# Features made one group ahead, a last step without modulation work, and another chain for the norm's scale, in a two-layer decoder trunk

## The chip, the cores and the metric

The kernel runs on one core of a Trainium2 chip. The metric is the device time of one execution, in microseconds. The engines are TensorE (PE in the rows; PEld is its weight load), VectorE (DVE), ScalarE (ACT), GpSimd (POOL) and SyncE (SP), which here issues the transfers.

## What is computed

A decoder trunk of two layers for 256 tokens of 2048 features, in fp32. Each layer has two halves, a mixer (attention) and a squared-ReLU MLP with hidden size 8192. Both halves begin with an RMSNorm whose output is scaled and shifted by a vector that depends on the condition `c`, and end in a residual add with a gate that depends on `c` as well. Cut to this, the reference is:

```python
cond = jax.nn.silu(c)
for i in range(DEPTH):
    mod = cond @ ada_w[i] + ada_b[i]          # ada_w[i] is 2048 x 12288
    sh1, sc1, g1, sh2, sc2, g2 = [m[:, None, :] for m in jnp.split(mod, 6, axis=-1)]
    h = rms_norm(x, norm_mix_g[i]) * (1.0 + sc1) + sh1
    ...
    x = x + g1 * y                            # y: even_mixer or odd_mixer of h
    h = rms_norm(x, norm_mlp_g[i]) * (1.0 + sc2) + sh2
    x = x + g2 * (jnp.square(jax.nn.relu(h @ mlp_up[i])) @ mlp_down[i])
return rms_norm(x, final_norm_g)
```

## The kernel before

`xT` keeps the residual with features on partitions: 16 slices of 128 features by 256 tokens. Every product with a weight matrix is made of three fp32r matmuls. A weight block (`load`, 128 x 1024 elements, 512 KB) is split on the core into a high part `wh` (ACT, L319) and a low part `wl` (DVE, L321); activations are kept as a high and a low part as well (`xs` for a normed input, `hs` for others). Eight buffers hold blocks on their way in, four each hold `wh` and `wl`.

`make_h` (L459) makes the normed features of some slices, three instructions a slice: a product `t` of `xT`, the modulated norm weight and the norm's scale `R` on DVE (L463), its shifted high part on ACT (L464), the low part on DVE (L465).

The modulation vectors come from `ada_w`, a matrix as large as the MLP's. `queue` lines up its column sections in `fill`; `ada` is a generator that does one step for each `pump`: it loads one 512 KB block and accumulates it into a row, on DVE (L242, L245) or, for a few sections, on TensorE (L238). After a section's last step its row is put into `late`, one entry for each 512 columns: four TensorE transposes (L263), a DVE reduction (L265) and small DVE instructions (L272, L275) that write `mod`. `tick`, called with nearly every weight load, first does one entry of `late`, then adds `2 * rate[0]` to a credit and pumps once for each whole unit. `need(left, keys)` pumps until at most `left` sections of the keys are queued, and empties `late`.

The even mixer's input projection (`even`, L615) can't wait for the whole modulation. It runs in five feature groups (`K1_GROUPS`, L39) of 2, 2, 4, 4 and 4 slices. For a group it calls `need`, then `make_h`, and then nine projections with `kproj` (L374): one of keys and values held in two `bank` tiles of PSUM, then pairs for `qb`, `qa`, `ka`, `va`. Partial sums of a group are copied out by ACT (L402) and copied back into PSUM for the next one (L383). The rates of the groups stand in `R_K1` (L41). `up_streamed` (L671) does the same for the first half of the up projection of layer 0: four groups of 4 slices, eight projections each.

`down` (L499) makes output projections in four blocks of 512 features and four steps of 512 rows. With `residual` (L477) it adds into `xT` and, for the next norm, squares each slice on ACT (L147) and adds it on DVE into `sacc` (L151); the last square is kept apart. `sumsq` (L440) sums over features by TensorE, `rstd` (L433) takes the power -0.5 on POOL (L437), and `norm_scale` (L448) spreads the result over all partitions: DVE scales an identity matrix by it (L453), TensorE multiplies by ones (L454) into `R` in PSUM, and ACT copies it to `Rs` in SBUF if `keep` (L456). `Rs` is the same tile as `sacc`.

In layer 1 the features of a norm are made lazily: `lazy_h` (L470) puts four calls of `make_h` into `hgen`, and the first `proj` (L348) after it takes one for each step of 512 rows.

The framework works out waits between engines from the tiles that instructions touch and sets each engine's order of instructions by its own estimates; `tc.issue_after(i)` puts what a block issues behind instruction `i` on its engine.

Of the kernel before, what the change touches and what calls it, by code (L numbers as in the profile page):

```python
# [15 lines left out]
ALU = mybir.AluOpType  # L16
# [24 lines left out]
R_K1 = (0.6, 0.75, 0.9, 0.9, 1.6)  # L41
# [41 lines left out]
def build(tc, consts, x, c, norm_mix_g, norm_mlp_g, ada_w, ada_b, mlp_up, mlp_down, even_w_in, even_sinks,  # L83
# [5 lines left out]
    with ctx:  # L89
# [258 lines left out]
        def proj(W, c0, outs):  # L348
            Ps = []
            off = 0  # L350
            for kind, n, ev in outs:
                Ps.append((off, [mm_tile() for _ in range(n // 128 if kind == "T" else 2)]))
                off += n
            for g in range(4):
# [5 lines left out]
                tick()  # L360
                for (kind, n, ev), (o, P) in zip(outs, Ps):
# [78 lines left out]
        def sumsq():  # L440
            ps = aux()
            sq = last.pop()
            for j in range(2):
                T.matmul(ps[:, j:j + 1], sacc[:, 128 * j:128 * j + 128], ones[:, 0:1], start=True, stop=False)
                T.matmul(ps[:, j:j + 1], sq[:, 128 * j:128 * j + 128], ones[:, 0:1], start=False, stop=True)
            return ps[:, 0:2]

        def norm_scale(ss, keep=True):  # L448
            r = rstd(ss)
            R = aux()  # L450
            dg = t256()
            for j in range(2):
                V.tensor_scalar(dg[:, 128 * j:128 * j + 128], ident, r[:, j:j + 1], None, op0=ALU.mult)  # L453
            T.matmul(R[:, 0:S], ones, dg, start=True, stop=True)  # L454
            if keep:
                A.activation(Rs, R[:, 0:S], AF.Copy)  # L456
            return R[:, 0:S]

        def make_h(l, sh, sc, R, ks=range(KT)):  # L459
            for k in ks:  # L460
                t = t256()
                b = mod[:, 6 * l + sh, k:k + 1]
                V.scalar_tensor_tensor(t, xT[:, k, :], mod[:, 6 * l + sc, k:k + 1], R, op0=ALU.mult, op1=ALU.mult)  # L463
                ia = A.activation(xs[:, k, 0:S], t, AF.Identity, bias=b)  # L464
                iv = V.scalar_tensor_tensor(xs[:, k, S:2 * S], t, b, xs[:, k, 0:S].bitcast(F32), op0=ALU.add, op1=ALU.subtract)  # L465
            return ia, iv
# [3 lines left out]
        def lazy_h(l, sh, sc, R):  # L470
            for g in range(4):
                hgen.append(lambda g=g: make_h(l, sh, sc, R, range(4 * g, 4 * g + 4)))
# [26 lines left out]
        def down(W, row0, tiles, order, ev, lazy=None):  # L499
            for blk in range(4):  # L500
                P = [mm_tile() for _ in range(4)]
                for n, g in enumerate(order):
                    ws = load(W, row0 + 512 * g, 4, 512 * blk, 512)
                    tick()
# [27 lines left out]
        def mlp(l, first=0, us=None):  # L532
            ys = []
            for ch in range(first, 4):
# [24 lines left out]
                down(mlp_down[l], 2048 * ch, tiles, range(4), residual(l, 5, True, l == 1) if ch == 3 else partial(l, ys, ch))  # L559
# [55 lines left out]
        def even():  # L615
# [24 lines left out]
            held = [bank() for _ in range(2)]  # L640
            for g, (k0, kn) in enumerate(K1_GROUPS):
                end = len(K1_GROUPS) - 1
                need(end - g, (0, 1))
                ia, iv = make_h(0, 0, 1, Rs, range(k0, k0 + kn))
# [303 lines left out]
```

## Time and profile before

| what | value |
| --- | --- |
| median of 3 runs | 2288.84 us (2287.96 to 2292.45) |
| the profiled execution | 2290.15 us |
| its span, first to last instruction | 2288.4 us |
| PE busy | 2216.7 us, 97% |
| DVE busy | 1662.1 us, 73% |
| ACT busy | 1180.4 us, 52% |
| moved by DMA | 600.06 MB, mean 262 GB/s |

The windows below give, for a stretch, the busy time of each engine and in brackets its number of instructions, the clock that was granted to TensorE as a share of 2.4 GHz, the busy share of the DMA engines and what they moved. Matmuls are pipelined and their ends are modelled, so their count in a stretch says more than their busy time.

### The profile page before, as it was taken

To read this page: it belongs to the slowest core of one execution; us is meant where nothing else is said; L and a number is where in the kernel's file an instruction comes from. 1 tells how busy PE (TensorE), PEld (TensorE's weight loads), DVE (VectorE), ACT (ScalarE), POOL (GpSimd) and SP (SyncE) were. 2 spreads that over 40 slices of the span, in tenths; PEclk is the share of its full clock that TensorE was granted. 3 is DMA by queue.
4 is the path that set the end of the run, shared out by engine and by line. 5 is a ranking of instruction groups with operands and counts; after the bars stand their busy time and mean duration, and the time that the engine had idled before them with its cause. 6 is when DMAs were issued, how large, how long until landed. Compare 5 with 4: busy or idle time off the path is not lost.

```text
span 2288.4 us, 45838 instructions
## 1 busy us (share of the span) xinstructions
PE 2216.7 (97%) x18602; PEld 2147.1 (94%) x18602; DVE 1662.1 (73%) x2341; ACT 1180.4 (52%) x1873; POOL 5.6 (0%) x25
## 2 busy tenths in 40 slices
PE   8899999899999999999999999999999999999998
PEld 4799889899999999999999989899999999999997
DVE  3887899988877788887777977887545555555555
ACT  3766974578844354354454555444444444443543
POOL 0000000000000000000000000000000000000000
PEclk9999999999999999999999999999999999999999
DMA  9999679999998988988858876985555656555652
GB/s 320 312 333 322 242 258 364 326 355 364 328 317 276 319 290 300 312 306 295 262 184 296 313 253 222 325 313 159 193 198 190 199 190 201 188 198 189 199 185 93
DMA packets 296246, 600.06 MB, mean 262 GB/s; under 512 B 24706, under 2 KB 41954, under 8 KB 296034
## 3 DMA queue, kind: packets, MB, share of 16 engines
q1 hardware_dynamic: 295488, 596.38, 76.5%
q8 instruction: 146, 2.39, 0.4%
q10 hardware_dynamic: 546, 0.75, 0.1%
q14 instruction: 66, 0.54, 0.1%
HBM read 594.95 MB, written 2.10 MB: 261 GB/s over the span
## 4 chain that ended last, share of the span: by engine, by line
PE 47%; issue 33%; DVE 8%; DMA 7%; ACT 4%; SPq 0%; DVEq 0%; POOLq 0%; POOL 0%; ACTq 0%
PE mm L333 30%; PE mm L399 12%; DMA wa<-in_ada_w_dram 5%; DVE wl L321 3%; DVE acc L245 2%; PE bank L399 1%; ACT wh L319 1%; DMA w<-in_odd_w_in_dram 1%; PE row L238 1%; DMA w<-in_even_w_in_dram 1%; PE cps L263 1%; ACT u L402 1%; ACT mm L383 0%; PE bank L605 0%; ACT hs L417 0%
## 5 line engine op out<-in xcount | busy, mean ns | idle before, releaser
L321 DVE TENSOR_TENSOR wl<-w,wh 128x1024 fp32r<-128x1024 f32 x736 | 881.6, 1221 | 421.3 <-ACT wh L319 417.2
L319 ACT ACTIVATE wh<-w 128x1024 fp32r<-128x1024 f32 x736 | 754.1, 1055 | 771.4 <-PE mm L333 666.6
L333 PE MATMUL mm<-hs,wh 128*128 128x256 f32 x5120 | 881.3, 277 | 0.4 <-DVE xT L481 0.4
L333 PEld LDWEIGHTS mm<-hs,wh 128*128 128x128 f32 x5120 | 772.6, 188 | 1.6 <-DVE xT L481 1.0
L333 PE MATMUL mm<-xs,wh 128*128 128x256 f32 (+1 forms) x4128 | 717.8, 279 | 3.1 <-ACT xs L464 3.0
L333 PE MATMUL mm<-hs,wl 128*128 128x256 f32 x2560 | 708.3, 277 | 4.1 <-DVE wl L321 4.1
L333 PEld LDWEIGHTS mm<-xs,wh 128*128 128x128 f32 (+1 forms) x4128 | 626.3, 188 | 6.4 <-ACT xs L464 4.5
L333 PE MATMUL mm<-xs,wl 128*128 128x256 f32 x2064 | 571.7, 278 | 0.4 <-DVE wl L321 0.3
L245 DVE SCALAR_TENSOR_TENSOR acc<-wa,cond,acc 128x1024 f32<-128x1024 f32 x330 | 423.1, 1282 | 98.1 <-DMA wa<-in_ada_w_dram 96.3
L333 PEld LDWEIGHTS mm<-hs,wl 128*128 128x128 f32 x2560 | 481.0, 188 | 5.1 <-DVE wl L321 4.9
L333 PEld LDWEIGHTS mm<-xs,wl 128*128 128x128 f32 x2064 | 387.6, 188 | 1.5 <-DVE wl L321 1.0
L399 PE MATMUL mm<-xs,wh 128*128 128x256 f32 x1792 | 315.2, 280 | 6.0 <-ACT wh L319 4.2
L399 PEld LDWEIGHTS mm<-xs,wh 128*128 128x128 f32 x1792 | 273.2, 190 | 16.4 <-ACT wh L319 5.4
L399 PE MATMUL mm<-xs,wl 128*128 128x256 f32 x896 | 249.1, 279 | 1.5 <-DVE wl L321 1.5
L399 PEld LDWEIGHTS mm<-xs,wl 128*128 128x128 f32 x896 | 169.2, 190 | 2.2 <-DVE wl L321 2.1
L402 ACT ACTIVATE u<-mm 128x512 f32<-128x512 f32 x144 | 84.1, 592 | 73.9 <-PE mm L399 73.0
L383 ACT ACTIVATE mm<-u 128x512 f32<-128x512 f32 x112 | 65.5, 597 | 1.2
L548 ACT ACTIVATE t<-mm 128x256 f32<-128x256 f32 x96 | 36.5, 380 | 31.5 <-PE mm L333 26.2
L147 ACT ACTIVATE t<-xT 128x256 f32<-128x256 f32 x60 | 24.6, 415 | 51.3 <-DVE xT L481 51.3
L577 ACT ACTIVATE p<-p,st 128x128 f32<-128x128 f32 (+1 forms) x96 | 40.1, 420 | 19.7 <-DVE st L591 10.0
L399 PE MATMUL mm<-wh,xs 128*128 128x256 f32 x256 | 49.4, 286 | 0.1
L343 PE MATMUL mm<-wh,xs 128*128 128x256 f32 (+1 forms) x128 | 43.7, 342 | 0.0
(213 smaller groups left out, 1408.4 us busy)
## 6 DMA issues: line engine op xcount, KB each, us to landing
wa<-in_ada_w_dram SPq DMA_DIRECT2D x256, 512.0 KB, 5.2
w<-in_mlp_up_dram SPq DMA_DIRECT2D x256, 512.0 KB, 4.4
w<-in_mlp_down_dram SPq DMA_DIRECT2D x256, 512.0 KB, 4.9
wa<-in_ada_w_dram SPq DMA_DIRECT2D x256, 256.0 KB, 5.1
w<-in_odd_w_in_dram SPq DMA_DIRECT2D x88, 512.0 KB, 4.7
w<-in_even_w_in_dram SPq DMA_DIRECT2D x72, 512.0 KB, 5.4
w<-in_even_w_out_dram SPq DMA_DIRECT2D x32, 512.0 KB, 5.7
w<-in_odd_w_out_dram SPq DMA_DIRECT2D x32, 512.0 KB, 5.5
```

Of the source, the lines that this page charges most:

```text
L147: A.activation(s, xT[:, kt, :], AF.Square)
L238: T.matmul(row[q:q + 32, :], cond[:, k:k + 1].to_broadcast([128, 32]), w[:, i, :], start=k < 4, stop=k >= KT - 4, tile_position=(0, q))
L245: V.scalar_tensor_tensor(acc, w[:, i, :], cond[:, k:k + 1], acc, op0=ALU.mult, op1=ALU.add)
L319: A.activation(wh, w, AF.Copy)
L321: V.tensor_tensor(wl, w, wh.bitcast(F32), op=ALU.subtract)
L333: T.matmul(P[0:m, 0:S], st[:, c0:c0 + m], mv, start=f and i == 0, stop=e and i == 2)
L343: T.matmul(Ps[j][:, 0:n], lo, wh[:, c0:c0 + n], start=False, stop=e)
L383: A.activation(P, flat[i], AF.Copy)
L399: T.matmul(Ps[i][:, 256 * h:256 * h + 256], st, mv, start=first and e == 0, stop=last and e == 2, skip_group_check=True)
L402: A.activation(flat[i], P, AF.Copy)
L548: A.activation(r, P[:, 0:S], AF.Relu)
L577: A.activation(p[:, o:o + n], p[:, o:o + n], AF.Exp, bias=m[:, i:i + 1], accum_out=den[:, i:i + 1])
```

## The change

- `even` and `up_streamed` get a function `features(g)` with the `need` and the `make_h` of a group. Group 0's is called first. Group g+1's is called inside group g: in `even` before the last two projections (`ka`, `va` of b = 1) of a 2-slice group, before the last (`va`) of a 4-slice group; in `up_streamed` before the eighth.
- The first two rates of `R_K1` become 0.65 and 0.9.
- `down` takes `sums`; where a sum of squares follows, the last step of the last block calls no `tick`.
- `sumsq` multiplies both halves of `sacc` first, then both halves of the last square, as one accumulation.
- `norm_scale` no longer scales an identity on DVE: TensorE takes the broadcast result of POOL as the stationary operand, against the identity. The copy to `Rs` is always made, and layer 1's groups after the first read `Rs`.
- `make_h` puts each product from the third on behind the low part two slices before it.
- In the first `proj` after `lazy_h`, the first step goes slice by slice through its four output tiles, and no longer tile by tile through its four slices.

```diff
-R_K1 = (0.6, 0.75, 0.9, 0.9, 1.6)
+R_K1 = (0.65, 0.9, 0.9, 0.9, 1.6)
...
+            fresh = len(hgen) == 4
             for g in range(4):
...
                 tick()
+                if fresh and g == 0:
+                    for k in range(4):
+                        for mt in range(4):
+                            mm_T(Ps[0][1][mt], ws[k:k + 1], 128 * mt, 128, xs_rhs(k, 1), k == 0, False)
+                    continue
...
         def sumsq():
             ps = aux()
             sq = last.pop()
-            for j in range(2):
-                T.matmul(ps[:, j:j + 1], sacc[:, 128 * j:128 * j + 128], ones[:, 0:1], start=True, stop=False)
-                T.matmul(ps[:, j:j + 1], sq[:, 128 * j:128 * j + 128], ones[:, 0:1], start=False, stop=True)
+            for t in (sacc, sq):
+                for j in range(2):
+                    T.matmul(ps[:, j:j + 1], t[:, 128 * j:128 * j + 128], ones[:, 0:1], start=t is sacc and j == 0, stop=t is sq and j == 1,
+                             skip_group_check=True)
...
-        def norm_scale(ss, keep=True):
+        def norm_scale(ss):
             r = rstd(ss)
             R = aux()
-            dg = t256()
             for j in range(2):
-                V.tensor_scalar(dg[:, 128 * j:128 * j + 128], ident, r[:, j:j + 1], None, op0=ALU.mult)
-            T.matmul(R[:, 0:S], ones, dg, start=True, stop=True)
-            if keep:
-                A.activation(Rs, R[:, 0:S], AF.Copy)
+                T.matmul(R[:, 128 * j:128 * j + 128], r[:, j:j + 1].to_broadcast([128, 128]), ident, start=True, stop=True)
+            A.activation(Rs, R[:, 0:S], AF.Copy)
...
         def make_h(l, sh, sc, R, ks=range(KT)):
+            done = []
             for k in ks:
                 t = t256()
                 b = mod[:, 6 * l + sh, k:k + 1]
-                V.scalar_tensor_tensor(t, xT[:, k, :], mod[:, 6 * l + sc, k:k + 1], R, op0=ALU.mult, op1=ALU.mult)
+                with tc.issue_after(done[-2]) if len(done) > 1 else nullcontext():
+                    V.scalar_tensor_tensor(t, xT[:, k, :], mod[:, 6 * l + sc, k:k + 1], R, op0=ALU.mult, op1=ALU.mult)
...
+                done.append(iv.ins)
...
-                hgen.append(lambda g=g: make_h(l, sh, sc, R, range(4 * g, 4 * g + 4)))
+                hgen.append(lambda g=g: make_h(l, sh, sc, Rs if g else R, range(4 * g, 4 * g + 4)))
...
-        def down(W, row0, tiles, order, ev, lazy=None):
+        def down(W, row0, tiles, order, ev, lazy=None, sums=True):
...
-                    tick()
+                    if not (sums and blk == 3 and n == 3):
+                        tick()
...
+            def features(g):
+                need(end - g, (0, 1))
+                k0, kn = K1_GROUPS[g]
+                return make_h(0, 0, 1, Rs, range(k0, k0 + kn))
+
+            ia, iv = features(0)
             for g, (k0, kn) in enumerate(K1_GROUPS):
-                end = len(K1_GROUPS) - 1
-                need(end - g, (0, 1))
-                ia, iv = make_h(0, 0, 1, Rs, range(k0, k0 + kn))
...
                     kproj(W, g, 512 * b, [(256 * i, "T", qa[b][i]) for i in range(2)], k0, kn)
+                    if b == 1 and g < end and kn == 2:
+                        features(g + 1)
                     kproj(W, g, 1024 + 512 * b, [(256 * i, "T", ka[b][i]) for i in range(2)], k0, kn)
...
+                    if b == 1 and g < end and kn == 4:
+                        features(g + 1)
                     kproj(W, g, 2048 + 512 * b, [(0, j, va[b][j]) for j in range(2)], k0, kn)
...
                 for b in range(4 * K2C):
+                    if g < 3 and b == 4 * K2C - 1:
+                        features(g + 1)
```

## Rows read from the trace of the kernel before

**Rows 1.** The page's first part: busy time, share of the span and instructions of each engine.
```profile
PE 2216.7 (97%) x18602; PEld 2147.1 (94%) x18602; DVE 1662.1 (73%) x2341; ACT 1180.4 (52%) x1873; POOL 5.6 (0%) x25
```
**Rows 2.** Windows over the second and third group of the up projection of layer 0: stretch, its length, busy time of each engine with its instructions, granted clock, DMA share, GB/s.
```profile
467.20:510.80 43.60, 43.60 (x387) 43.60 (x387) 39.10 (x44) 35.32 (x52) 0.00 (x0) 1.00 0.98 342
510.80:554.40 43.60, 43.60 (x387) 43.60 (x386) 39.11 (x43) 34.32 (x52) 0.00 (x0) 1.00 0.99 366
```
**Rows 3.** Windows over the even projection: group 1, and the turns to groups 2, 3 and 4.
```profile
61.00:102.00 41.00, 34.46 (x269) 32.66 (x268) 33.32 (x35) 31.48 (x50) 0.00 (x0) 0.96 0.97 340
102.00:112.00 10.00, 5.46 (x30) 5.23 (x29) 10.00 (x19) 6.28 (x11) 0.00 (x0) 0.66 0.74 241
...
158.00:170.00 12.00, 8.41 (x49) 8.17 (x48) 9.98 (x18) 6.32 (x11) 0.00 (x0) 0.72 0.79 270
...
217.00:224.00 7.00, 5.16 (x30) 1.88 (x29) 6.48 (x14) 4.47 (x8) 0.00 (x0) 1.00 0.52 183
```
**Rows 4.** Windows over the norms after the even output projection, the first MLP and the odd output projection, and over a stretch of the first MLP.
```profile
411.80:426.00 14.20, 8.08 (x37) 6.82 (x36) 12.52 (x23) 4.71 (x9) 1.62 (x1) 0.64 0.84 305
1137.80:1150.00 12.20, 8.44 (x44) 7.73 (x44) 8.81 (x20) 5.59 (x11) 1.28 (x13) 0.72 0.21 28
...
1565.00:1577.00 12.00, 8.24 (x43) 7.22 (x42) 8.38 (x20) 5.50 (x11) 0.69 (x1) 0.72 0.11 33
...
690.00:703.00 13.00, 9.80 (x75) 9.61 (x74) 10.71 (x20) 7.79 (x18) 0.00 (x0) 0.87 0.52 177
```
**Rows 5.** Waits of PE over the whole span: what waited for what, us in total, times, longest.
```profile
PE bank L399 <- ACT xs L464: 10.8, 4, 4.5
...
PE mm L333 <- ACT xs L464: 3.0, 3, 1.1
```
**Rows 6.** Timeline of DVE, PE and ACT around the turn to group 2, in order of time: start, duration (of all in a merged row), engine, line, operation, count, and in square brackets the idle time before and what ended it.
```profile
96.41 2.60 DVE L245 SCALAR_TENSOR_TENSOR acc<-wa,cond,acc 128x1024 f32<-128x1024 f32 x2
...
101.64 1.04 PE L263 MATMUL cps<-cst,acc 128*128 128x128 f32 x8
...
102.93 1.28 DVE L265 TENSOR_REDUCE s<-cps 128x4 f32<-128x512 f32 x2
...
104.20 1.22 DVE L321 TENSOR_TENSOR wl<-w,wh 128x1024 fp32r<-128x1024 f32 x1
...
106.14 1.27 DVE L463 SCALAR_TENSOR_TENSOR t<-xT,mod,sacc 128x256 f32<-128x256 f32 x3
...
106.66 1.31 ACT L464 ACTIVATE xs<-t,mod 128x256 fp32r<-128x256 f32 x3 [1.98 <-DVE t L463]
...
107.22 0.58 PE L399 MATMUL bank<-xs,wh 128*128 128x256 f32 x1 [4.54 <-ACT xs L464]
```
**Rows 7.** The last weight block of group 1: the timeline of the DMA queue (SPq), the transfers between 60 and 102 us by name (size, median us from issue to landing), and the timeline of ACT.
```profile
83.48 0.38 SPq L316 DMA_DIRECT2D w<-in_even_w_in_dram  x1
...
w<-in_even_w_in_dram SPq DMA_DIRECT2D x12, 512.0 KB, 5.4
...
94.19 1.04 ACT L319 ACTIVATE wh<-w 128x1024 fp32r<-128x1024 f32 x1
```
**Rows 8.** Timeline of all engines at the norm after the even output projection.
```profile
411.06 1.28 DVE L245 SCALAR_TENSOR_TENSOR acc<-wa,cond,acc 128x1024 f32<-128x1024 f32 x1
...
411.81 0.28 PE L333 MATMUL mm<-hs,wl 128*128 128x256 f32 x1
...
413.38 1.28 DVE L245 SCALAR_TENSOR_TENSOR acc<-wa,cond,acc 128x1024 f32<-128x1024 f32 x1
...
415.14 0.35 PE L444 MATMUL aux<-cst,sacc 128*128 128x1 f32 x2 [3.06 <-DVE sacc L151]
...
416.70 1.23 DVE L321 TENSOR_TENSOR wl<-w,wh 128x1024 fp32r<-128x1024 f32 x1
416.86 1.62 POOL L437 TENSOR_TENSOR s<-s 128x2 f32<-128x2 f32 x1 [401.50 <-DVE s L435]
...
420.37 0.38 ACT L456 ACTIVATE sacc<-aux 128x256 f32<-128x256 f32 x1 [5.51 <-PE aux L454]
420.79 1.26 DVE L463 SCALAR_TENSOR_TENSOR t<-xT,mod,aux 128x256 f32<-128x256 f32 x3 [0.60 <-ACT sacc L456]
```
**Rows 9.** Timeline of all engines at the norm after the first MLP.
```profile
1137.84 0.28 PE L333 MATMUL mm<-hs,wl 128*128 128x256 f32 x1
...
1138.66 0.35 PE L444 MATMUL aux<-cst,sacc 128*128 128x1 f32 x2 [0.55 <-DVE sacc L151]
...
1139.42 0.38 PE L445 MATMUL aux<-cst,t 128*128 128x1 f32 x2 [0.40 <-ACT t L147]
1139.66 0.36 PE L444 MATMUL aux<-cst,sacc 128*128 128x1 f32 x2
1139.88 0.36 PE L445 MATMUL aux<-cst,t 128*128 128x1 f32 x2
...
1140.59 0.69 POOL L437 TENSOR_TENSOR s<-s 128x2 f32<-128x2 f32 x1 [722.12 <-DVE s L435]
...
1141.32 0.48 DVE L453 TENSOR_SCALAR t<-cst,s 128x128 f32<-128x128 f32 x2 [0.87 <-POOL hs L423]
1141.94 0.67 PE L454 MATMUL aux<-t,cst 128*128 128x256 f32 x2 [1.70 <-DVE t L453]
1142.65 1.26 DVE L463 SCALAR_TENSOR_TENSOR t<-xT,mod,aux 128x256 f32<-128x256 f32 x3 [0.85 <-PE aux L454]
```

More of the change, by code (lines that the diff above doesn't have):

```diff
@@ L558, in mlp @@
                     need(0, (l, 5))
-                down(mlp_down[l], 2048 * ch, tiles, range(4), residual(l, 5, True, l == 1) if ch == 3 else partial(l, ys, ch))
+                down(mlp_down[l], 2048 * ch, tiles, range(4), residual(l, 5, True, l == 1) if ch == 3 else partial(l, ys, ch), sums=ch == 3)
         def p_tile():
@@ L640, in even @@
             held = [bank() for _ in range(2)]
+            end = len(K1_GROUPS) - 1
+            def features(g):
[3 more added lines that the diff above has]
+            ia, iv = features(0)
             for g, (k0, kn) in enumerate(K1_GROUPS):
-                end = len(K1_GROUPS) - 1
-                need(end - g, (0, 1))
-                ia, iv = make_h(0, 0, 1, Rs, range(k0, k0 + kn))
                 rate[0] = R_K1[g]
@@ L672, in up_streamed, with features @@
             us = [u_tile() for _ in range(8 * K2C)]
+            def features(g):
+                need(3 - g, (l, 4))
+                return make_h(l, 3, 4, Rs if g else R, range(4 * g, 4 * g + 4))
+            ia, iv = features(0)
             for g in range(4):
-                need(3 - g, (l, 4))
-                ia, iv = make_h(l, 3, 4, Rs if g else R, range(4 * g, 4 * g + 4))
                 for b in range(4 * K2C):
+                    if g < 3 and b == 4 * K2C - 1:
+                        features(g + 1)
                     if g == 0 and b == 2 and GATE:
@@ L909, in build @@
         need(0, (1, 0))
-        lazy_h(1, 0, 1, norm_scale(sumsq(), False))
+        lazy_h(1, 0, 1, norm_scale(sumsq()))
         rate[0] = R_ODD
@@ L915, in build @@
         need(0, (1, 3))
-        lazy_h(1, 3, 4, norm_scale(sumsq(), False))
+        lazy_h(1, 3, 4, norm_scale(sumsq()))
         rate[0] = R_M1
```

## The prediction, written before the changed kernel was run

> **What bounds the kernel now.** I read the page's shares first: TensorE (PE) is busy 97% of the span [rows 1], so an edit pays only where PE stands idle or runs at its lower clock. The yardstick is the up projection of layer 0, where PE issues 387 matmuls in 43.6 us, 8.88 per us, with no idle time at granted clock 1.00 [rows 2]. A stretch with fewer has lost its length less count/8.88. I then cut the even projection and the norms into windows. Feature group 1 and its end (61 to 102 us) hold 269 matmuls, 30.3 us of work in 41: 10.7 lost. The turn to group 2 (102 to 112) holds 30: 6.6 lost. The turn to group 3 (158 to 170) holds 49: 6.5 lost. The turn to group 4 (217 to 224) is filled with modulation matmuls, and PE idles 1.84 [rows 3]. At the norms the same count gives 10.0 lost at norm 1 (after the even output projection), 7.2 at norm 2 (end of the first MLP) and 7.2 at norm 3 (end of the odd output projection) [rows 4]. These places and group 1 make up nearly 50 us. The waits of PE name the turn's cause: the first matmul of a group, into `bank`, waits for the features that ACT writes (L464), 10.8 us in four waits [rows 5]. The timeline of the turn shows the chain: last modulation step on DVE, transposes on PE at 101.64, DVE reductions at 102.93, a weight conversion in between at 104.20, the first product at 106.14, ACT's feature at 106.66, PE at 107.22 [rows 6]. The windows add that the granted clock is 0.66 and 0.72 at the two turns, between the 1.2 and 2.4 GHz levels, so each idle stretch is paid again at the lower level.
>
> **Part 1: features made ahead in the even projection.** `features(g+1)` stands before the last two projections of a 2-slice group and before the last of a 4-slice group. Nothing is added on DVE, ACT or PE; `need`, the transposes, the reductions, 2 or 4 L463/L464/L465 triples move. The chain from transposes to the first feature took 107.22 - 101.64 = 5.6 us [rows 6]; one 4-slice projection is 48 matmuls, 5.4 us, and two 2-slice ones are as long, and in groups 2 and 3 one of the two transposes comes a projection earlier still. So the chain is covered to within 0.2 us, and I take the whole of the two turns and the idle part of the third: 6.6 + 6.5 + 1.84 = 14.9, less 0.3. That the mode can run is shown by the up projection: same 48-matmul projections, same rate 0.9, features of later groups ready early, no idle PE, at 342 and 366 GB/s [rows 2].
>
> What is queued behind it: the transposes now stand in PE's queue before the last projections, and those wait if the accumulator is late. Counting `tick`s by the rates, the 8th, 24th and 40th step after the start (each the last one that groups 1, 2 and 3 need) come in the 7th tick of their group, 56 in the 7th of group 3, so `need` pumps nothing. Before, the accumulator of the turn was done at 99.0 and its transposes came at 101.64 [rows 6], 2.6 us of slack; both move together.
>
> The price is in the rates. 60 steps instead of 56 are issued by the end of group 3, each a 524 KB transfer and a 1.2 us DVE instruction. In groups 2 and 3 DVE and the queue have room (the up projection again). In group 1 the transfers set the pace: DMA share 0.97 at 340 GB/s [rows 3], so one block costs 0.524/0.340 = 1.54 us. The last weight block of group 1 is the 52nd block of the queue instead of the 48th, 4 x 1.54 = 6.2 us later. It was issued at 83.48 and takes about 5.4 to land, 88.9, and its conversion came at 94.19 [rows 7]: 5.3 us of slack. Shown cost 0.9; bounds 0 (slack holds) and 6.2 (none holds). I take 2, nearer the slack row, since DVE and ACT are also nearly full there (33.3 and 31.5 of 41 us) [rows 3]. **Part 1: 14.6 - 2 = 12.6, bounds 6 and 16.**
>
> **Part 2: features made ahead in the up projection.** PE has no idle time there [rows 2]: 0, cover is the projection it stands before.
>
> **Part 3: no modulation in the last step of a sum of squares.** At norm 1 the two accumulations at 411.06 and 413.38 stand between the last residuals; `sacc` is read at 415.14 [rows 8]. PE's last projection matmul starts at 411.81, so 3.3 us pass; at norm 2, with no accumulation there, the same step takes 0.8 (1137.84 to 1138.66) [rows 9]. Gain 2.5. The two steps are only later, in the up projection, where DVE has 4.5 us per 43.6 to spare. Norms 2 and 3 had none in the way: 0.
>
> **Part 4: the norm chain.** (a) Sums: both `sacc` matmul pairs go first, so of the three pairs from 1139.42 on [rows 9] two are left after the last square: 0.22 less. (b) The two DVE scalings at 1141.32 go; PE takes the POOL result itself. POOL ends at 1141.28 and PE's R matmul starts at 1141.94 [rows 9]; 0.6 less, with two shorter matmul pairs in place of one, no change taken. (c) `R` is now copied for layer 1 too. At norm 1 DVE's first product (420.79) starts only after ACT's copy ends (420.37 + 0.38), while at norm 2 without the copy it follows PE's R directly (1142.65) [rows 8, 9]: 0.4 more at norms 2 and 3.
> The Trainium skill (PSUM — Partial Sum Buffer, "PSUM bank collisions raise a hardware error") says that two engines must not read one bank and quadrant at once and that a dependency is put between them. That speaks against this copy; the trace agrees at norm 1, and by the rule norms 2 and 3 gain 0.4 each from the chain, without it 0.8.
> (d) POOL's power took 1.62 beside a DVE conversion (416.70) and 0.69 beside an idle DVE [rows 8, 9]. The conversions stay, so I take no gain; bound 0.9.
> The Trainium skill (GPSIMD Engine Reference, "1. Specifications") says that POOL shares its SBUF interfaces with DVE instructions of two SBUF inputs. By that rule the 0.9 is gained at norm 1 only if no conversion falls beside the power.
> (e) k-outer order in the first projection of a `lazy_h` (`fresh`) and low parts interleaved by `issue_after`: PE's waits for features at L333 are 3.0 us in three [rows 5]; restarts run at the lower clock, where PE needs them more slowly. Gain 0 to 3, I take 1.2 in both norms together.
>
> Norm 1: gap 2.5 + 0.2 + 0.6 = 3.3. PE restarts earlier and may spend more of its first work at the lower level: bounds 1.5 and 6. Norms 2 and 3: 2 x 0.4 + 1.2 = 2.0, bounds -0.5 and 4. The final norm keeps its chain: 0.
>
> **Sum.** 12.6 + 3.3 + 2.0 = 17.9; bounds 7 and 26. The profiled execution is 2290.15 (span 2288.4, 1.75 around it): 2272. It is 1.3 above the median of the three runs, less than their spread of 4.5.
>
> **Rivals.**
> A, DVE takes PE's place at the turns. In the last projection's 5.4 us DVE gets four products and four differences (0.4 each, 3.2), a reduction (0.6), two conversions (2.3) and two accumulations (2.4): 8.5. Without a lead 3.1 is missing at each of two turns, and with the 6.2 of group 1 there remain 14.6 - 6.2 - 6.2 + 5.3 = 7.5: 2283. For it: 33.3 of 41 busy in group 1. Against: the up projection carries the same load with PE full.
> B, the change doesn't do what it says. The order on an engine isn't the program's (a conversion stands between reduction and product at 104.20 [rows 6]); if the features stay late, part 1 gives 0 less 2 of group 1: 2290.15 + 2 - 5.3 = 2287.
> C, slower: TensorE waits inside the groups. If transfers set the pace up to group 4, the transposes stand before matmuls that could have run, and the last weights come 6.2 us later; the turns' gain is gone, and the norms' is eaten by the copy (2 x 0.4) and by low clock: 2290.15 + 6.2 + 0.8 = 2297. It decides if accumulators come more than 2.6 us later relative to PE and the weights' 5.3 us of slack are used up.
> D, more: the power at 0.69 (0.9), group 1 at no price (2), part 4e at its bound (1.8), and a 4.6 us loss in the first MLP (690 to 703: 75 matmuls in 13 us [rows 4]), which hangs on where a modulation step falls, goes away: 2272.2 - 9.3 = 2263.
>
> **How the numbers follow.** Forecast 0.62 (2265 to 2281), D 0.08, A 0.15 (2281 to 2286), B 0.08 (2286 to 2291), C 0.07. 0.2% is 4.6 us, about what a measurement can tell from no change. Faster: 0.62 + 0.08 + two thirds of A = 0.80; same: 0.05 + 0.08 = 0.13; slower 0.07. The range 2258 to 2286 takes in the forecast, A and most of D, and leaves out B and C.
>
> **What would show it.** Right: no wait of a `bank` matmul for L464 over 1 us, granted clock near 1.00 through the turns, group 4 starting near 209 instead of 221.8; 1 us or less from the last matmul to `sacc` at norm 1; no DVE instruction between the power and PE. Wrong: PE waits for L263's accumulator or for conversions before the last projection of groups 1 to 3 (A, C); L463 still right ahead of the group's first matmul (B); norms 2 and 3 no shorter, because of the copy.

## The result and the profile after

The changed kernel takes 2301.77 us (median of 5, 2300.13 to 2305.47) where the kernel before takes 2288.84 beside it (median of 5, 2286.04 to 2294.68): ratio 1.0052 [1.0036, 1.0069]. It is 0.5% slower, by the interval clear of no change; 2272 was forecast. The profiled execution took 2305.47, the slowest of the five; its span is 2303.6.

Page, first part (answers to [rows 1]): PE's share is the same, in a span 15 us longer.
```profile
PE 2225.7 (97%) x18610; PEld 2153.0 (93%) x18610; DVE 1660.4 (72%) x2333; ACT 1182.9 (51%) x1875; POOL 5.1 (0%) x25
```
Windows over groups 1, 2 and 3, each from its first matmul, then over the turns to groups 2, 3 and 4 (answer to [rows 3]; columns as there). PE is busy at the turns to groups 2 and 3: 66 and 68 matmuls in place of 30 and 49, at granted clock 0.94 and 1.00. But group 1 runs at 0.84, and group 3 takes 62 us.
```profile
69.00:112.00 43.00, 34.09 (x224) 31.75 (x223) 33.01 (x38) 27.39 (x44) 0.00 (x0) 0.84 0.90 310
112.00:167.00 55.00, 51.92 (x444) 51.15 (x444) 47.68 (x50) 38.34 (x58) 0.00 (x0) 1.00 0.95 337
167.00:229.00 62.00, 59.19 (x482) 52.52 (x480) 43.31 (x44) 40.90 (x59) 0.00 (x0) 1.00 0.96 341
...
108.00:118.00 10.00, 8.54 (x66) 8.13 (x65) 8.90 (x11) 8.83 (x14) 0.00 (x0) 0.94 0.75 238
162.00:172.00 10.00, 8.15 (x68) 7.85 (x67) 9.81 (x13) 8.48 (x13) 0.00 (x0) 1.00 0.87 272
225.00:232.00 7.00, 5.04 (x33) 3.88 (x34) 5.92 (x12) 3.37 (x7) 0.00 (x0) 1.00 1.01 384
```
Waits of PE from 61 to 230 us: who waits for whom, us in total, times, longest. The `bank` matmuls' wait for features [rows 5] is gone from this stretch. In its place come waits for weight conversions and for a modulation row.
```profile
PE mm L405 <- DVE wl L321: 6.1, 9, 1.8
PE mm L405 <- ACT wh L319: 5.4, 3, 2.1
PE cps L263 <- ACT acc L249: 2.3, 1, 2.3
```
The same view of before, 61 to 224 us: conversions cost 6.4 there, 11.5 after.
```profile
PE bank L399 <- ACT xs L464: 9.0, 3, 4.5
PE mm L399 <- ACT wh L319: 4.2, 2, 2.1
PE mm L399 <- DVE wl L321: 2.2, 4, 0.8
```
Timeline of the end of group 3 in after, PE and ACT. After the last projection matmul (222.02) PE does 16 row matmuls (L238), then waits for ACT's copy of a row, which stands behind two weight conversions, then does eight transposes. Group 4's first matmul comes 7 us after group 3's last.
```profile
222.02 0.28 PE L405 MATMUL mm<-wh,xs 128*128 128x256 f32 x1
...
222.22 1.92 PE L238 MATMUL row<-wa,cond 128*32 128x512 f32 x16
...
223.96 1.99 ACT L319 ACTIVATE wh<-w 128x1024 fp32r<-128x1024 f32 x2
...
225.86 0.58 ACT L249 ACTIVATE acc<-row 128x512 f32<-128x512 f32 x1
...
226.49 1.10 PE L263 MATMUL cps<-cst,acc 128*128 128x128 f32 x8 [2.34 <-ACT acc L249]
...
229.03 0.67 PE L405 MATMUL bank<-xs,wh 128*128 128x256 f32 x2
```
Timeline of norm 1 in after (answer to [rows 8]). From the last matmul (424.87) to the one that reads `sacc` (427.37) 2.5 us pass; the prediction's sign was 1 or less. Two conversions stand there now. An accumulation (L242) runs beside POOL's power (L443).
```profile
424.87 0.28 PE L333 MATMUL mm<-hs,wl 128*128 128x256 f32 x1
...
425.76 1.22 DVE L321 TENSOR_TENSOR wl<-w,wh 128x1024 fp32r<-128x1024 f32 x1
...
427.23 1.22 DVE L321 TENSOR_TENSOR wl<-w,wh 128x1024 fp32r<-128x1024 f32 x1
...
427.37 0.61 PE L451 MATMUL aux<-cst,sacc 128*128 128x1 f32 x4 [1.78 <-DVE sacc L151]
...
428.54 0.75 DVE L242 TENSOR_SCALAR acc<-wa,cond 128x1024 f32<-128x1024 f32 x1
428.70 1.15 POOL L443 TENSOR_TENSOR s<-s 128x2 f32<-128x2 f32 x1 [413.05 <-DVE s L441]
```
Timeline of norm 2 in after (answer to [rows 9]). The R matmuls follow POOL directly (1151.36 + 0.69, then 1152.11). The first product now waits for ACT's copy (1152.85 + 0.38, then 1153.27).
```profile
1148.83 0.28 PE L333 MATMUL mm<-hs,wl 128*128 128x256 f32 x1
...
1151.36 0.69 POOL L443 TENSOR_TENSOR s<-s 128x2 f32<-128x2 f32 x1 [721.52 <-DVE s L441]
...
1152.11 0.71 PE L459 MATMUL aux<-cst,s 128*128 128x128 f32 x4 [1.09 <-POOL hs L429]
1152.85 0.38 ACT L460 ACTIVATE sacc<-aux 128x256 f32<-128x256 f32 x1 [2.50 <-PE aux L459]
1153.27 0.87 DVE L469 SCALAR_TENSOR_TENSOR t<-xT,mod,aux 128x256 f32<-128x256 f32 x2 [2.06 <-ACT sacc L460]
...
1154.35 0.58 PE L333 MATMUL mm<-xs,wh 128*128 128x256 f32 x1 [1.53 <-ACT xs L470]
```
The table divides each run's profiled span by landmarks read from its timeline: the first matmul of group 4, and for each norm PE's last matmul before it and the first after it. "W1" is the work from group 4 to norm 1, "W2" and "W3" lead to norms 2 and 3, "N" are the gaps, "end" is what follows norm 3. The runs themselves are told further down. One profile's stage wanders by some 3 us where nothing was changed (group 4 starts at 221.8 in before, 219.9 in e_g4_more and 223.0 in e_m0_more, whose code is the same up to there). Each row is one execution, and that lies up to 4.9 us from its run's median (e_lead_back 2289.85, median 2294.73). So what a part costs is taken from the ratios; the table shows where the time goes.

| kernel | group 4 at | W1 | N1 | W2 | N2 | W3 | N3 | end | span |
| --- | --- | --- | --- | --- | --- | --- | --- | --- | --- |
| before | 221.8 | 190.0 | 10.1 | 715.9 | 5.9 | 421.3 | 6.2 | 717.2 | 2288.4 |
| after | 229.0 | 195.9 | 7.6 | 716.3 | 5.5 | 425.7 | 5.6 | 718.0 | 2303.6 |
| e_rates_only | 228.3 | 197.5 | 8.7 | 709.5 | 5.9 | 419.3 | 6.4 | 716.5 | 2292.1 |
| e_even_only | 227.1 | 195.5 | 8.8 | 708.7 | 5.9 | 420.0 | 6.4 | 716.2 | 2288.6 |
| e_rest_only | 221.9 | 193.5 | 9.9 | 714.1 | 6.0 | 423.8 | 5.7 | 718.3 | 2293.2 |
| e_lead_back | 218.3 | 191.8 | 9.0 | 714.2 | 5.5 | 425.2 | 5.7 | 718.4 | 2288.1 |
| e_sums_back | 228.9 | 195.5 | 8.0 | 713.0 | 5.5 | 420.2 | 6.0 | 717.3 | 2294.4 |
| e_g4_more | 219.9 | 202.4 | 8.1 | 713.0 | 6.4 | 422.1 | 6.4 | 717.0 | 2295.3 |
| e_m0_more | 223.0 | 191.1 | 10.5 | 744.0 | 6.4 | 413.4 | 6.4 | 716.4 | 2311.2 |
| e_lead_back_m0 | 219.7 | 191.5 | 10.3 | 737.2 | 5.5 | 416.3 | 5.4 | 717.3 | 2303.2 |
| e_norm_only | 223.3 | 193.7 | 8.4 | 716.0 | 6.1 | 423.3 | 5.9 | 717.7 | 2294.4 |
| e_even_lead_back | 220.6 | 191.0 | 9.2 | 718.0 | 5.9 | 421.8 | 6.4 | 716.8 | 2289.7 |
| e_lead_back_sums | 220.4 | 191.7 | 8.3 | 716.8 | 5.5 | 422.0 | 5.5 | 718.4 | 2288.6 |
| e_turn34 | 213.8 | 199.5 | 10.0 | 715.4 | 6.0 | 420.5 | 5.8 | 717.6 | 2288.6 |
| e_hold_only | 219.5 | 193.4 | 9.2 | 714.5 | 6.4 | 422.9 | 6.1 | 717.4 | 2289.4 |
| e_norm_no_hold | 220.2 | 190.2 | 9.3 | 716.7 | 5.5 | 422.6 | 6.0 | 715.7 | 2286.2 |
| e_norm_no_fresh | 220.0 | 193.6 | 8.3 | 717.2 | 5.5 | 420.4 | 6.0 | 717.2 | 2288.2 |
| e_all_no_hold | 219.2 | 191.7 | 8.3 | 717.9 | 6.0 | 421.5 | 5.5 | 715.4 | 2285.5 |
| e_after_no_hold | 229.2 | 195.2 | 8.4 | 716.9 | 5.5 | 421.5 | 5.5 | 716.5 | 2298.7 |
| e_no_hold_ticks_back | 229.0 | 195.2 | 8.1 | 711.3 | 5.8 | 419.5 | 5.5 | 716.8 | 2291.2 |

Before against after: 13.1 lost up to norm 1 (7.2 + 5.9), 2.5 won at N1, 4.4 lost in the odd mixer (W3), 1.0 won at N2 and N3, 0.4 and 0.8 lost in W2 and at the end.

The even projection by groups, each from its first matmul to the next group's first, in us:

| kernel | group 0 | group 1 | group 2 | group 3 |
| --- | --- | --- | --- | --- |
| before | 37.0 | 40.6 | 56.5 | 58.1 |
| after | 38.7 | 43.3 | 54.8 | 61.8 |
| e_rates_only | 37.2 | 42.5 | 54.5 | 63.5 |
| e_even_only | 37.2 | 44.3 | 51.7 | 64.0 |
| e_lead_back | 37.1 | 43.3 | 54.6 | 53.7 |
| e_turn34 | 37.0 | 40.4 | 52.5 | 53.4 |

### The profile page after: what moved, and what is told of

Read it like the earlier page. It is cut to its first block, busy times and chain, and to the rows that moved or that the text cites. A ratio compares the mean times of both kernels' runs of the same rounds, so it can differ in the third digit from the quotient of the medians.

```text
span 2303.6 us, 45828 instructions
## 1 busy us (share of the span) xinstructions
PE 2225.7 (97%) x18610; PEld 2153.0 (93%) x18610; DVE 1660.4 (72%) x2333; ACT 1182.9 (51%) x1875; POOL 5.1 (0%) x25
## 4 chain that ended last, share of the span: by engine, by line
PE 49%; issue 33%; DVE 7%; DMA 6%; ACT 3%; SPq 0%; POOL 0%; DVEq 0%; POOLq 0%; ACTq 0%
PE mm L333 31%; PE mm L405 13%; DMA wa<-in_ada_w_dram 5%; DVE wl L321 3%; DVE acc L245 2%; PE bank L405 1%; ACT wh L319 1%; PE row L238 1%; PE cps L263 1%; PE bank L613 1%; DMA w<-in_even_w_in_dram 0%; ACT u L408 0%; DMA w<-in_odd_w_in_dram 0%; PE bank L589 0%; ACT t L416 0%
## 5 line engine op out<-in xcount | busy, mean ns | idle before, releaser
L245 DVE SCALAR_TENSOR_TENSOR acc<-wa,cond,acc 128x1024 f32<-128x1024 f32 x330 | 422.9, 1281 | 93.8 <-DMA wa<-in_ada_w_dram 91.6
L405 PE MATMUL mm<-xs,wh 128*128 128x256 f32 x1792 | 319.9, 282 | 6.1 <-ACT wh L319 3.3
L405 PEld LDWEIGHTS mm<-wh,xs 128*128 128x128 f32 x256 | 41.9, 197 | 4.6 <-ACT wh L319 2.3
```

Of the source, the lines that this page charges most:

```text
L245: V.scalar_tensor_tensor(acc, w[:, i, :], cond[:, k:k + 1], acc, op0=ALU.mult, op1=ALU.add)
L405: T.matmul(Ps[i][:, 256 * h:256 * h + 256], st, mv, start=first and e == 0, stop=last and e == 2, skip_group_check=True)
```

## The experiments

Ratios are to the kernel before, run beside each group of runs (medians 2291.63 to 2292.73).

**First: halves of the change.** The parts are: the early features of the even projection, the lead (four modulation steps more by the end of group 3, by `R_K1`), the withheld ticks (`sums`), the norm chain. e_even_only is before with the new `even()` and the new rates; e_rates_only has the rates alone; e_rest_only is after with `even()` and rates of before; e_lead_back is after with the last two rates lower:
```
-R_K1 = (0.65, 0.9, 0.9, 0.9, 1.6)
+R_K1 = (0.65, 0.9, 0.9, 0.8, 1.45)
```


> The kernel before with the new even projection (features made ahead there) and the two new rates, nothing else of the change. The profiles show the loss up to the out projection: the changed kernel is 12.5 us behind there. Theories M (the four modulation steps that the rates bring ahead cost time) and F (the features inside a group delay weight conversions) both expect 10 to 15 us slower than before, 2299 to 2304. Rival R (the norm edits and the order they bring cost it) expects 0 to 4 us faster than before.

> The kernel before with the two new rates alone; features stay at the turns. Theory M: four steps more by the end of group 3 put tensor-made steps into group 3 (3.5 us of TensorE) and DVE-made ones into group 4 (4.8 us of DVE), and lengthen group 1: 6 to 12 us slower than before. Theory F: within 2 us of before.

> The changed kernel with the even projection and the rates of before: the norm chain, the step without modulation work and the up projection's early features alone. Theories M and F: 2 to 5 us faster than before, the norms' gaps shorter by 2.3, 0.4 and 0.5 us. Rival R: 2 us or more slower than before, with the loss between norms 2 and 3.

> The changed kernel with the last two rates lowered to 0.8 and 1.45, so that the lead of four steps is gone by the end of group 4 (92 steps instead of 97 there, 93 in the kernel before). Theory M: 5 to 8 us faster than the changed kernel, with 18 or so modulation matmul instructions in group 3 again instead of 34. Theory F: within 2 us of the changed kernel.

Measured: e_even_only 1.0005 [0.9989, 1.0022], e_rates_only 1.0006 [0.9988, 1.0024], e_rest_only 1.0013 [0.9999, 1.0028], e_lead_back 1.0009 [0.9992, 1.0025]. For the first two, theory M's totals are missed; e_rest_only came out in total as rival R had it; e_lead_back is 9.9 us below the changed kernel, more than theory M's 5 to 8. No half has the loss alone; the parts interact. The rates alone reproduce the late start (228.3 + 197.5), and early features change nothing in it. But the kernel with the rates alone gets 8.4 back in W2 and W3; the whole change gets none back.

The rates alone also fill the turns. In e_rates_only the features stand at the turns as before, and yet no `bank` matmul waits for them: the first product of group 2 is at 104.89, 5.4 us before the group's first matmul (1.1 in before [rows 6]). Waits of PE from 61 to 230 us, then windows over the turns to groups 2 and 3:
```profile
PE mm L399 <- ACT wh L319: 5.4, 3, 2.1
PE mm L399 <- DVE wl L321: 4.5, 10, 0.8
PE cps L263 <- ACT acc L249: 2.3, 1, 2.3
PE bank L399 <- DVE wl L321: 2.1, 4, 0.8
```
```profile
106.00:116.00 10.00, 8.76 (x65) 8.34 (x65) 9.22 (x12) 9.51 (x16) 0.00 (x0) 0.92 0.82 265
160.00:170.00 10.00, 9.36 (x77) 8.92 (x76) 9.67 (x13) 8.45 (x15) 0.00 (x0) 1.00 0.91 314
```
With the rates the same in both, early features are worth nothing that the runs can tell (1.0005 and 1.0006).

With the lead given back, group 3 is what the forecast wanted: the window over it shows PE without a gap at full clock.
```profile
164.60:218.30 53.70, 53.70 (x462) 50.97 (x460) 42.34 (x45) 39.46 (x59) 0.00 (x0) 1.00 0.96 339
```
In after, e_rates_only, e_even_only and e_no_hold_ticks_back, which carry the lead, 34 row matmuls (L238) and 12 transposes (L263) stand in group 3; in this one 20 and 8.

**Second: where a modulation step falls.** Edits: the tick put back (e_sums_back), one rate raised in the kernel before (`R_M0 = 0.75` in e_m0_more, the last of `R_K1` at 1.85 in e_g4_more), and e_lead_back with `R_M0 = 0.75` (e_lead_back_m0).
```
-                    if not (sums and blk == 3 and n == 3):
-                        tick()
+                    tick()
```


> The changed kernel with the modulation tick put back into the last step of each sum of squares; early features, new rates and the new norm chain stay. Theory W (where a modulation step falls sets the time; the withheld ticks only push steps into the second half of the odd mixer, where DVE is the bound, and there each costs about 1.2 us): the start is as late as in the changed kernel (out projection near 322, norm 1 near 424), but the odd mixer gets 4 to 6 us back, so about 2296. Theory R (the three edits are bad each by itself and add): withheld ticks are a gain of 2.5 at norm 1, so without them 2302 or later.

> The kernel before with the last rate alone higher, R_K1 = (0.6, 0.75, 0.9, 0.9, 1.85): 5 more modulation steps in feature group 4 and its attention, none more in groups 0 to 3. Theory W with the price in group 4 (DVE nearly full there): group 4 starts at 222 as before, the out projection starts 5 x 1.2 = 6 us later, near 316, and PE waits near its start for an accumulator. If the price of the lead sat in group 3 (row matmuls and the accumulator's wait there), the out projection stays near 310.

> The kernel before with R_M0 = 0.75 in place of 0.6: some 29 modulation steps are done in the first MLP that would else fall into the odd mixer. Theory W: the first MLP has room on DVE (norm 1 to norm 2 stays at 716 or grows by under 5 us), the odd mixer and its projection lose some 20 fewer steps in the stretch where DVE is the bound and go from 421 to about 400; total about 2270. Theory R (transfers or PE set the pace in the MLP, DVE does not set it in the odd mixer): norm 1 to norm 2 grows by as much as the odd mixer loses, 29 x 1.5 = 40 us of transfers at most; total 2288 or more.

> The changed kernel with R_K1 = (0.65, 0.9, 0.9, 0.8, 1.45) and R_M0 = 0.75: early features with the lead given back in groups 3 and 4, and the modulation of the odd mixer's second half done in the first MLP. Theory W: the start is that of the run with the lead given back alone (group 4 near 218, norm 1 near 410), and the odd mixer's stretch is shorter by up to 20 us: 2270 to 2285, faster than the kernel before. Theory R: 2294, no faster than with the lead given back alone.

e_sums_back: 1.0011 [0.9998, 1.0024], theory W's 2296 (2296.27). W2 and W3 are 3.3 and 5.5 shorter than in after, N1 only 0.4 longer. In W2 a stall that after has at 708, as before has it at 697 [rows 4], nearly goes with the ticks back and the lead kept. It does not hang on the ticks alone: e_lead_back_sums has its ticks and has it (3.4). In W3 after does as many accumulations as before (86), and e_sums_back 83; why W3 is 4.4 longer than before is open. Waits of PE at the stall, first after (706 to 716 us), then e_no_hold_ticks_back (699 to 714; a run told below).
```profile
PE mm L333 <- DVE wl L321: 3.3, 1, 3.3
```
```profile
PE mm L333 <- DVE hs L424: 0.9, 1, 0.9
PE mm L333 <- DVE wl L321: 0.3, 1, 0.3
```
e_g4_more (2297.13, one run): five more steps in group 4 and its attention and nothing else make W1 12.4 longer, where 6 would be five accumulations of 1.2. The trace of W1 has 7.9 us more DVE work: four accumulations, two reductions and what comes with them. The whole span is 6.9 longer, since N1 and W2 are shorter. The first out-projection matmul, which the expectation named, was issued at 311 and hid it. The waits of PE in this stretch show where most of it goes (7.2): attention's matmuls wait for the probabilities of DVE and ACT. Before (222 to 312 us), e_g4_more (220 to 322), e_lead_back (218 to 310):
```profile
PE bank L605 <- ACT pt L583: 1.6, 3, 0.8
PE bank L581 <- DVE p L598: 1.3, 1, 1.3
```
```profile
PE bank L605 <- ACT pt L583: 5.6, 6, 1.9
PE bank L581 <- DVE p L598: 4.5, 2, 2.5
```
```profile
PE bank L613 <- ACT pt L591: 1.1, 3, 0.5
...
PE bank L589 <- DVE p L606: 0.2, 1, 0.2
```
e_m0_more (2313.02, one run) and e_lead_back_m0 (1.0053 [1.0032, 1.0074]) refute theory W's price of 1.2 a step in the odd mixer. 29 steps moved into the first MLP make W2 28.1 longer (0.97 each) and W3 7.9 shorter (0.27 each). So the first MLP has no room at rate 0.6, and what the withheld ticks cost is not the number of steps left over alone. Whether DVE or the transfers set the 0.97 is not shown. Windows from norm 1 to norm 2, before and e_m0_more: DVE gets 37 us more work, and PE's matmuls stay nearly the same.
```profile
411.80:1137.80 726.00, 715.69 (x6244) 712.84 (x6243) 594.65 (x682) 385.62 (x546) 1.62 (x1) 0.99 0.91 313
```
```profile
414.10:1168.60 754.50, 729.85 (x6260) 720.38 (x6259) 631.56 (x719) 384.92 (x546) 1.62 (x1) 0.99 0.92 321
```
**Third: parts alone.** e_norm_only: before with the norm chain, `make_h` and the first projection of after. e_even_lead_back: before with the new `even()` and the rates of e_lead_back. e_lead_back_sums: e_lead_back with the tick back. e_turn34: features ahead only from 4-slice groups:
```
+                if g and K1_GROUPS[g - 1][1] == 2:
+                    ia, iv = features(g)
                 rate[0] = R_K1[g]
...
-                    if b == 1 and g < end and kn == 2:
-                        features(g + 1)
```


> The kernel before with the edits of the norm chain alone: sums in the other order, PE takes the result of POOL itself, the copy also for layer 1, make_h with issue_after, the other order of the first projection. Features, rates and ticks are those of before. The prediction's part 4 gives 2.6 us less (0.6 + 0.2 at norm 1, 1.8 at norms 2 and 3): 2290. Rival (the chain is 0.4 shorter at each norm, but the moved copy and order cost elsewhere, as the run with the ticks back against the run with the early features alone makes it look, 2.2 us): 2295. Where it is the first, the odd mixer starts 1 to 2 us earlier than in before; where it is the second, the difference shows between norm 1 and norm 2, and the gaps themselves are no longer than before.

> The kernel before with the early features of the even projection and R_K1 = (0.65, 0.9, 0.9, 0.8, 1.45), nothing else: ticks and norm chain are those of before. Theory W (the lead must be given back before the attention of the even mixer, and the steps must not pile up in the second half of the odd mixer): group 4 starts near 218, norm 1 near 410, and the odd mixer, with 2 steps fewer done than in before, loses 1 to 2 us there: 2288, about 4 below the kernel before. Rival: the early features bring nothing that lasts, 2293.

> The changed kernel with the last two rates at 0.8 and 1.45 and with the tick back in the last step of the sums: all of the change but the withheld ticks and the lead in groups 3 and 4. Theory W: the start of the run with the lead given back (norm 1 near 411), 3 to 4 us less lost in the odd mixer than there: 2291. If the withheld ticks cost nothing: 2295, as with the lead given back alone.

> The kernel before with early features only for the groups that follow a 4-slice group (3 and 4), features of groups 1 and 2 at the turn as before, R_K1 = (0.6, 0.75, 1.0, 0.9, 1.45): 48 steps by the end of group 2 as the last feature needs them, no lead in groups 0 and 1. Theory W with the price of the lead of group 1 (5 to 9 us of late weights there): group 2 starts at 107 as in before, the turn to group 3 loses under 2 us in place of 6, group 4 starts near 216, 2287. Rival (the weights of group 1 are late, but the steps done there make the next turns shorter, so nothing is gained by leaving it out): group 4 starts at 218 or later, 2290 or more.

Measured: e_norm_only 1.0018 [1.0006, 1.0031]; e_even_lead_back 0.9978 [0.9965, 0.9991]; e_lead_back_sums 0.9998 [0.9988, 1.0009]; e_turn34 1.0003 [0.9993, 1.0014]. Early features with the lead given back are a gain of 5 us by the ratio; adding the norm edits and the up projection's features takes it away again, and the norm edits alone cost 4. Whether the 5 us come from the early features is not shown: no run has these rates with the features at the turns, and with the rates of the change early features gained nothing. e_turn34 is a miss for theory W. Its group 3 is as short (53.4), group 4 starts at 213.8, earliest of all, but W1 takes 199.5: what is won before group 4 is lost in it. Which wait does that is open; attention's waits in W1 (3.8 and 1.8 where before has 2.2 and 1.3) and one of 2.5 for a conversion cover under half of the 9.5 by which W1 is longer.

**Fourth: the hold.** In the changed kernel `make_h` issues each product behind the low part two slices before (`issue_after`). The edit takes this hold out:
```
             for k in ks:
...
-                with tc.issue_after(done[-2]) if len(done) > 1 else nullcontext():
-                    V.scalar_tensor_tensor(t, xT[:, k, :], mod[:, 6 * l + sc, k:k + 1], R, op0=ALU.mult, op1=ALU.mult)
+                V.scalar_tensor_tensor(t, xT[:, k, :], mod[:, 6 * l + sc, k:k + 1], R, op0=ALU.mult, op1=ALU.mult)
```
e_hold_only has it without the rest, e_norm_no_hold is e_norm_only without it, e_norm_no_fresh is e_norm_only with `fresh = False`, e_all_no_hold is e_lead_back_sums without the hold.

> The kernel before with the hold in make_h alone (each product is issued after the low part two before it). Theory H (the hold opens gaps in DVE's order at the turns, into which conversions and accumulations are put ahead of the third and fourth product): the turns to groups 3 and 4 are 1 to 2 us longer, 2294 to 2296 in all. Rival N (the hold does nothing, the order of the first projection or the chain is the cause): 2291.6.

> The edits of the norm chain alone, without the hold. Theory H: the turn to group 3 is as in before (a wait of 3.9 in place of 4.8), 2289 to 2292, as the prediction's part 4 without its 1.2. Rival N: 2296, as with the hold.

> The edits of the norm chain alone, with the order of the first projection as before. Theory H: 2296, as with it (or 1 more). If the order (k outside, four tiles in turn) is the cause: 2291, and the difference shows in the 5 us behind norms 2 and 3.

> All of the change but the hold, the withheld ticks and the lead in groups 3 and 4 (R_K1 = 0.65, 0.9, 0.9, 0.8, 1.45). Theory H: 2287 or less, 4 less than with the hold, so below the kernel before as the early features alone were with these rates (0.9978), and norms 2 and 3 0.4 shorter each. Rival N: 2292.

Measured: e_hold_only 1.0011 [1.0002, 1.002]; e_norm_no_hold 0.998 [0.997, 0.9989]; e_norm_no_fresh 1.0014 [1.0003, 1.0025]; e_all_no_hold 0.9975 [0.9966, 0.9984]. Theory H's totals hold in all four, within 3 us: the hold costs, the order of the first projection does not, and both kernels without the hold beat the kernel before. The timelines at the turn to group 3, DVE without the hold (e_norm_no_hold) and with it (e_hold_only), show what it does: one more conversion goes ahead of the products, and an accumulation takes the third product's place.
```profile
159.60 1.23 DVE L321 TENSOR_TENSOR wl<-w,wh 128x1024 fp32r<-128x1024 f32 x1
...
160.94 1.27 DVE L468 SCALAR_TENSOR_TENSOR t<-xT,mod,sacc 128x256 f32<-128x256 f32 x3
```
```profile
159.30 1.23 DVE L321 TENSOR_TENSOR wl<-w,wh 128x1024 fp32r<-128x1024 f32 x1
...
160.51 1.22 DVE L321 TENSOR_TENSOR wl<-w,wh 128x1024 fp32r<-128x1024 f32 x1
...
161.65 0.87 DVE L465 SCALAR_TENSOR_TENSOR t<-xT,mod,sacc 128x256 f32<-128x256 f32 x2
...
162.44 1.28 DVE L245 SCALAR_TENSOR_TENSOR acc<-wa,cond,acc 128x1024 f32<-128x1024 f32 x1
```
The expected place was wrong: group 2's first matmul to group 4's takes 114.5 to 114.7 us with the hold at the turn (e_hold_only, e_norm_only, e_norm_no_fresh, e_rest_only), and 114.4 to 114.6 without (before, e_norm_no_hold, e_m0_more; 112.8 in e_g4_more). Most of the loss lies behind. W1 is 193.4 to 193.7 with the hold at the turn (e_hold_only, e_norm_only, e_norm_no_fresh, e_rest_only) and 190.0 to 191.1 without (before, e_norm_no_hold, e_m0_more): in the traces the order of DVE, ACT and PE differs from group 1 on, through the whole attention; which wait in W1 costs the 3 us is not shown. Behind norm 3 the hold costs 0.5 to 3.0 ("end" of the four pairs that also have the new order of the first projection). There PE waits for a late low part in after, e_norm_only, e_sums_back and e_lead_back_sums, and in none of their four partners without the hold:
```profile
PE mm L333 <- DVE xs L471: 0.5, 1, 0.5
```
**Fifth: the whole change, taken down step by step.** The edits are those above: after without the hold, then also with the tick back.

> The changed kernel without the hold in make_h, nothing else. If the parts add: the hold cost 5.3 (ratio 0.9998 to 0.9975) and 8.7 (1.0018 to 0.998) in the two pairs run so far, so 1.0014 to 1.0029 of the kernel before, 2295 to 2299. If the hold costs nothing where features are made ahead in long groups with the lead: 2301 to 2305.

> The changed kernel without the hold and with the tick back in the last step of the sums; the lead of its rates stays. If the parts add: the ticks give 9 us (1.0052 to 1.0011, with the hold in both), so 0.9975 to 0.999, 2287 to 2291, and the lead is worth at most 3 against the run that also gives it back. If the lead is the larger part in this company: 2295 or more.

Measured: e_after_no_hold 1.003 [1.0019, 1.0042], just above where the sum of the parts had it (1.0014 to 1.0029), and e_no_hold_ticks_back 1.0007 [0.9994, 1.0019], where the sum had 0.9975 to 0.999. In this order the loss splits as 1.0052, 1.0030 (hold: 5.0 us), 1.0007 (withheld ticks: 5.3), 0.9975 (lead, e_all_no_hold: 7.3). In another order the shares shift: with the hold in, the ticks were worth 9.4 (1.0052 to 1.0011) and the lead 3.0 (to 0.9998). With the lead taken first it is worth 9.9 (1.0052 to 1.0009), and the ticks after it 2.5 (to 0.9998). That each of the three costs time is shown; how much depends on the order, and the shares are not additive. e_all_no_hold, 2285.66, is the fastest here: all of the change but these three, 5.7 us below the kernel before. That is hardly more than e_even_lead_back (5.0) or e_norm_no_hold (4.6) gains by itself, so the gains do not add either.

## Why the prediction was wrong, step by step

**What bounds it.** Right that PE's idle time at the turns was there and could be filled: no `bank` matmul waits for features behind group 0, and in e_lead_back group 3 takes 53.7 in place of 58.1. What failed is that this time was taken as won at the end. No row of the prediction lies between 224 and 411 us; W1 is full of DVE, ACT and PE work that depends on each other, and an earlier start is partly lost there (in e_turn34 all of 8).

**Part 1, 12.6 of the 17.9.** Three steps failed.

The first is "I take the whole of the two turns", less a price of 2 "with bounds 0 and 6.2" in group 1. From group 0's first matmul to group 2's first 77.6 us pass in before and 82.0 in after. It is 79.8 to 83.7 in the eleven kernels with the first two rates of the change, and 75.9 to 78.4 in the nine without. With the 6.6 that the turn was to give, the price in after is 11.0, beyond its bounds. (Part 1's own bounds of 6 and 16 do not follow from its terms, which give 8.4 and 14.6.) It came out as foreseen in kind: conversions late, 11.5 of waits for 6.4 up to group 4, granted clock 0.84 in group 1. Up to group 3's first matmul nothing is won: 134.0 in before, 133.2 to 137.0 in the eleven, where the forecast needs 123.

The second is that the early features fill the turns. In e_rates_only the four steps of lead do it without them, and by the ratios early features add nothing to that. The prediction took the lead for a price only.

The third is "in groups 2 and 3 DVE and the queue have room", and that the sum ended with group 3. The lead makes group 3 7 to 10 us longer (61.8 to 64.0 against 53.4 to 54.5): more row matmuls and the 2.3 wait stand between group 3 and group 4. The kernel then stays four steps ahead through W1, which costs 3.5 to 4.5 more in the four pairs that differ by the lead and have early features, 7.5 in e_rates_only against before. Nothing in the traces speaks against the counting of `tick`s; where the steps land was not asked.

**Part 2.** 0 was forecast. W2 is 715.9 and 716.3, but no run has this part alone, and the other parts move W2 by some 7 (708.7 in e_even_only).

**Part 3, withheld ticks, -2.5.** N1 is 2.5 shorter in after, but the tick is not the reason: with the tick back it is 8.0 (0.4 of gain), and in e_rest_only, which withholds it, 9.9. The prediction left the place of the two accumulations empty; in after two conversions stand there, and the step from the last matmul to `sacc` takes 2.5 in place of 3.3, not 0.8. N1 hangs on what falls beside it: 8.1 to 10.5 in the eight kernels with the norm chain of before, 7.6 to 10.3 in the twelve with the new one (means 9.3 and 8.7). "The two steps are only later, in the up projection" failed as well: by the ratios they cost 2.5 to 9.4 us over the whole run. In the two pairs with the lead the windows of W2 and W3 are shorter by 8.8 and 7.6 with the ticks back.

**Part 4.** (a) to (c) right: N2 and N3 are 0.4 and 0.6 shorter (0.4 forecast from these three), and the copy stands ahead of the product by 0.4. The Trainium skill (PSUM — Partial Sum Buffer, "PSUM bank collisions raise a hardware error") tells of a dependency that is added between two engines' instructions on one bank and quadrant, reads too. All three norms of after agree: ACT's copy of `R` ends at 431.41, 1153.23 and 1584.53, DVE's product starts at 431.44, 1153.27 and 1584.57. (d) POOL's power took 1.15 at norm 1 in after, 1.55 in e_sums_back and 1.62 in before, 0.69 with DVE idle at norm 2. In the first three it ends 0.55 us or a little more after the DVE instruction that ran when it began: L242 in after (to 429.29, the power to 429.85), a conversion in e_sums_back (429.05, 429.60) and in before (417.93, 418.48). The rule that the prediction takes from the Trainium skill (GPSIMD Engine Reference, "1. Specifications") agrees for the conversions, which have two SBUF inputs; as it stands there it does not cover L242, which reads one tensor. (e) failed: `issue_after`, costed as part of a gain of up to 3, is a loss in all five pairs (by the ratios 0.9, 2.5, 5.0, 5.3 and 8.7 us; the 0.9 is not clear of noise). Without it part 4 gives 4.6 (e_norm_no_hold, by its interval 2.5 to 6.9), and 2.8 was forecast (0.8 at norm 1 and 2.0).

**The rivals.** C (2297, chance 0.07) was nearest: the gain of the turns is gone by group 3's start, and TensorE waits for an accumulator and conversions at the end of group 3. It lacked the hold, the ticks' later price and the attention behind the lead; no rival has them. A is partly right: 6.1 of PE's waits from 61 to 230 us are for DVE's conversions, 2.2 before. B is refuted: features do come early (at the turn to group 2 the first is made at 105.54, 7.0 us before its matmul).

## What to carry over

In a kernel whose engines are all filled by a common background task, a step brought ahead or held back is not a saving; price it at the place where it lands, and read the windows of that place too. An ordering constraint on a few instructions moves the planner's order far beyond them, so it needs a run of its own. A change of several parts should be timed part by part, and a part that needs another (early features need the rates) against that other alone: here the rates filled the turns, and three parts lose.

## What the runs showed that was not expected

The five more steps of e_g4_more, put into a stretch with a chain of dependent small steps (attention), add 7.9 us of DVE work and make the stretch 12.4 us longer; 29 of them in the MLP, where DVE is busy 82%, cost 0.97 each there. And filling the turns did not remove the low clock but moved it. Before, the granted clock was 0.66 and 0.72 at the turns to groups 2 and 3 [rows 3] and 0.93 over group 1 with its turn (66 to 107 us). In after group 1 has 0.84, as in e_rates_only and e_lead_back; PE waits for conversions there, 8.8 us in nine waits, where before has 6.4 in six.
